# First stage of a transformer-block kernel: low parts of the split to VectorE, scaling and copies to ScalarE, modulation sums one column ahead

## The chip, the cores and the metric

The kernel runs on one core of one Trainium2 chip. The metric is the device time of one execution in microseconds; before the change the median of three runs is 741.49 us (740.28 to 741.51). Engines are named as in the profile: PE (TensorE matmul), PEld (its weight loads), DVE (VectorE), ACT (ScalarE), POOL (GpSimd) and SP (SyncE, which issues most transfers).

## The reference, cut to what matters

One transformer block on 512 tokens of width 1024, in float32. The change lies in the first lines: the modulation from `c`, the normalised input `u`, and the first part of the product with `w_in`.

```python
mod = jax.nn.silu(c) @ w_ada[l] + b_ada[l]
sh1, sc1, g1, sh2, sc2, g2 = [m[:, None, :] for m in jnp.split(mod, 6, axis=-1)]
u = layer_norm(x) * (1 + sc1) + sh1
qa, ka, va, qb, kc, vc, ksl, vsl, kw, vw, gl = jnp.split(u @ w_in[l], split_at, axis=-1)
...
u = layer_norm(x) * (1 + sc2) + sh2
```

`b_ada` holds the bias of the modulation; `1 + sc` and `sh` are a scale and a shift per channel of `u`.

## The kernel before, in words

All float32 products are made of split operands: a raw tile is copied to a rounded high part (`hi`, type fp32r, on ACT, line 256), the low part is `raw - hi` (line 257, on the engine that the caller names), and each product is three matmuls, high by high, high by low and low by high (`mm3`, lines 259 to 262).

**The start.** The vector `c` is loaded as a row, spread over 128 partitions by two matmuls (line 288) and put through Silu into `crow` (line 289). The same vector as columns, `ccol`, is loaded on ACT's queue (line 274) and put through Silu on ACT ahead of `crow` (line 290); `ccol` is used only much later, for `g1` and `g2`. The four token tiles of `x` (128 x 1024 each) get their statistics on DVE (`bn`, `ag`, lines 294 to 302), the power and the offset `nb` on POOL (lines 296, 310, 311), and are normalised in place on ACT (line 336); of the fourth tile, 384 of 1024 columns are done on DVE (line 334).

**The first stage** is the loop at line 372 over `KD = 8` columns `j` of 128 channels of `u`. For each column:

- `ada_cols(j)` (lines 344 to 355) loads the weights of the scale and the shift of these 128 channels as four tiles `ada` of 128 x 512 (256 KB each) and reduces each against a half of `crow` on DVE (line 351, CUSTOM_DVE_ANT_0 in the profile, with an accumulator read behind it). The two halves and the bias are added by line 353, once for the scale and once for the shift, and line 355 adds 1 to the scale.
- `w_first[j]` (128 x 792, 396 KB) is loaded to `wraw`, copied to `whi` on ACT, and its low part `wlo` is made on POOL (`split(w, wh, wl, P)`). `whi` and `wlo` have two buffers each, `wraw` four, `ada` sixteen.
- The normalised `x` is transposed on PE (`x_turn`, line 364, column 0 before the loop's body goes on, columns 1 to 7 within the turn of column 0). The PSUM result is copied to `xTs` on ACT for the even columns and on DVE for the odd ones (lines 367 and 369; `XA = (0, 2, 4, 6)`).
- DVE scales and shifts `xTs` with the column's scale and shift (line 387), ACT copies the result to the high part of `u` (line 256), and DVE makes the low part (line 257).
- PE does 24 matmuls of 256 columns into the banks `first` (line 398) and 12 of 280 columns into the banks `comp` (lines 260 to 262): 36 per column.

Behind the loop PE goes on with the banks `quad` (the rest of `w_in`), and ACT and DVE empty `first` and `comp`. A tile scheduler sets the order of each engine's instructions from the program, the pools and the semaphores; each engine works through its own list in order.

Of the kernel before, what the change touches and what calls it, by code (L numbers as in the profile page):

```python
# [10 lines left out]
F32 = mybir.dt.float32  # L11
# [95 lines left out]
def body(ctx, tc, nc, a, out, dbg=None):  # L107
# [27 lines left out]
    LU = 2  # L135
    TP = 832
    XO = 1
    XV = 1
    X3 = 384
    XW = 0  # L140
    XE = 1
    HP = 0
    FS = 1
    QS = 1
    XA = (0, 2, 4, 6)
    WM = (12, 10)
    PW = 1
    WF = 1
# [49 lines left out]
    def wraw(shape=(128, 1024)):  # L198
        return slot('wr', NR, list(shape), F32, 'wraw')
# [71 lines left out]
        load(xt[t], a['x'][128 * t:128 * t + 128, :])  # L271
    ident = const('ident', [128, 128], A)
    bcol = const('b_col', [128, 4, KD], A)
    ccol = const('ccol', [128, KD], A)
    nhalf = cst.tile([128, 1], F32, name='nhalf')
    V.memset(nhalf, -0.5)
    mone = cst.tile([128, 1], F32, name='mone')
# [8 lines left out]
    for h in range(2):  # L286
        pr = bank('tr', 'cb')
        T.matmul(pr, ones[0:1, :], c1[h][0:1, :], start=True, stop=True)
        A.activation(crow[:, 512 * h:512 * h + 512], pr, AF.Silu)
    A.activation(ccol, ccol, AF.Silu)  # L290

    def rstd_of(st):
        ag = cst.tile([128, 4], F32, name='ag', tag='ag', bufs=4)
# [20 lines left out]
    def warm(n):  # L314
        if n:
            pw = bank('acc', 'warm')
            for _ in range(n):
                T.matmul(pw[:, 0:128], ones, ones, start=True, stop=True)
    for t in range(NT):
        if HP & 1:  # L320
            ctx2 = ExitStack()
            ctx2.enter_context(tc.high_priority())
        y = xt[t]
        ag = stats(y)
        if t in N0P:
            P.tensor_scalar(y, y, ag[:, 0:1], ag[:, 3:4], op0=ALU.subtract, op1=ALU.mult)
        else:
            nb = offset_of(ag, P if NBP else V)
            cs = [slice(0, 1024)]
            if t == 3:  # L330
                cs = [slice(0, X3), slice(X3, 1024)]
                if XV:
                    c = cs.pop(0)
                    V.tensor_scalar(y[:, c], y[:, c], ag[:, 0:1], ag[:, 3:4], op0=ALU.subtract, op1=ALU.mult)
            for c in cs:
                A.activation(y[:, c], y[:, c], AF.Identity, bias=nb, scale=ag[:, 3:4])
        if HP & 1:
            ctx2.close()
    warm(WM[1])


    mod = cst.tile([128, 4, KD], F32, name='mod')

    def ada_cols(j):
        for s in range(2):
            part = cst.tile([128, 2], F32, name='part', tag='part', bufs=4)
            for h in range(2):
                hs = slice(512 * h, 512 * h + 512)
                w = to('ada', F32)
                load(w, a['ada_col'][j, s][:, hs])  # L350
                V.tensor_tensor_reduce(w, w, crow[:, hs], 1.0, 0.0, op0=ALU.mult, op1=ALU.add,
                                       accum_out=part[:, h:h + 1])
            V.scalar_tensor_tensor(mod[:, s, j:j + 1], part[:, 0:1], part[:, 1:2], bcol[:, s, j:j + 1],
                                   op0=ALU.add, op1=ALU.add)
        V.tensor_scalar_add(mod[:, 0, j:j + 1], mod[:, 0, j:j + 1], 1.0)


    _, uh, ul = u_parts()
# [2 lines left out]
    def x_turn(j):  # L361
        pt = bank('tr', 'xT')
        for t in range(NT):
            T.transpose(pt[:, 128 * t:128 * t + 128], xt[t][:, 128 * j:128 * j + 128], ident)
        xT.append(t2('xTs', F32))
        if j in XA:
            A.activation(xT[j], pt, AF.Copy)
        else:
            V.tensor_copy(xT[j], pt)
    accs = [[bank(tg, 'first') for _ in range(2)] for tg in ('acc', 's')]  # L370
    NC1 = 512 + 280
    for j in range(KD):
        if j == 0 and XW:
            w = wraw((128, NC1))
            load(w, a['w_first'][j])
        ada_cols(j)
        if j > 0 or not XW:
            w = wraw((128, NC1))
            load(w, a['w_first'][j])
        wh, wl = whl((128, NC1))  # L380
        if j == 0 and XE:
            x_turn(0)
        split(w, wh, wl, P)
        if j == 0 and not XE:
            x_turn(0)
        y = xT[j]
        V.tensor_scalar(y, y, mod[:, 0, j:j + 1], mod[:, 1, j:j + 1], op0=ALU.mult, op1=ALU.add)
        h_, l_ = uh[j], ul[j]
        split(y, h_, l_, V)
        terms = [[(h_, wh)], [(l_, wh)], [(h_, wl)]] if j == 0 and XO else [[(h_, wh), (h_, wl), (l_, wh)]]  # L390
        for term in terms:
            for i in range(2):
# [626 lines left out]
    def ada_late_cols(gap, which=(2, 3)):  # L1019
        for i in which:  # L1020
            for j in range(KD):
                w = wgem()
                load(w, a['ada_col'][j, i])
                yield gap
                V.tensor_tensor_reduce(w, w, crow, 1.0, 0.0, op0=ALU.mult, op1=ALU.add, accum_out=mod[:, i, j:j + 1])
            V.tensor_add(mod[:, i, :], mod[:, i, :], bcol[:, i, :])
            if i == 2:
                V.tensor_scalar_add(mod[:, 2, :], mod[:, 2, :], 1.0)

    def ada_row(s, out_, gap=None):  # L1030
        res = []
# [525 lines left out]
```

## Time and profile before

| what | before |
|---|---|
| median of three runs | 741.49 us (740.28 to 741.51) |
| the profiled execution's own time | 741.5 us |
| its span, first to last instruction | 739.4 us |
| PE busy, share of the span | 694.3 us, 94% |
| DVE busy | 469.7 us, 64% |
| ACT busy | 338.0 us, 46% |
| POOL busy | 297.1 us, 40% |
| mean granted TensorE clock | 0.99 of full speed |

The span is shorter than the execution's time by 2.1 us, which lie around the first and the last instruction. Busy time counts an instruction from its start to its end, so two that overlap in the pipeline count twice in a mean duration; the distance from one start to the next is what a row of equal instructions costs. A wait is shown as idle time in square brackets, with what ended it.

### The profile page before, as it was taken

What the parts mean: (1) busy time and instruction counts of PE and PEld (TensorE: products, weight loads), DVE (VectorE), ACT (ScalarE), POOL (GpSimd) and SP (SyncE); (2) the same over time, 40 slices, a digit from 0 to 9 for tenths busy, and PEclk for the clock granted to TensorE, in tenths of its full rate; (3) what the DMA queues carried; (4) which work ended last, traced back from release to release, by engine and by line L of the source; (5) the groups of instructions that cost most, each with busy time, mean ns of one, the idle gap of its engine ahead of it and who ended that gap; (6) DMA issues with size and microseconds to landing.
All of it is one profiled execution on the core that took longest, in us unless ns stands there. A gap on an engine that the chain in (4) does not pass through costs nothing.

```text
span 739.4 us, 10876 instructions
## 1 busy us (share of the span) xinstructions
PE 694.3 (94%) x3964; PEld 596.2 (81%) x3964; DVE 469.7 (64%) x969; ACT 338.0 (46%) x685; POOL 297.1 (40%) x303
## 2 busy tenths in 40 slices
PE   7889799999789988999999999999999999999995
PEld 6788678987678977878898888888888888888884
DVE  6998985666788699989854344464543443434336
ACT  4225575664557678963654333433433332223101
POOL 3334583937446628432202011011011147676216
PEclk7999999999999999999999999999999999999998
DMA  8952632134644003080102223344342225343002
GB/s 309 387 186 91 219 125 86 59 110 175 228 139 148 30 29 115 1 275 39 58 27 68 107 86 132 126 147 162 122 138 87 91 83 166 116 141 117 28 15 99
DMA packets 29149, 89.93 MB, mean 122 GB/s; under 512 B 3748, under 2 KB 4516, under 8 KB 29096
## 3 DMA queue, kind: packets, MB, share of 16 engines
q1 hardware_dynamic: 28516, 89.05, 34.6%
q8 instruction: 31, 0.51, 0.3%
q10 hardware_dynamic: 580, 0.19, 0.1%
q14 instruction: 22, 0.18, 0.1%
HBM read 87.13 MB, written 2.10 MB: 121 GB/s over the span
## 4 chain that ended last, share of the span: by engine, by line
PE 50%; DVE 3%; POOL 1%; issue 1%; ACT 0%; POOLq 0%; DVEq 0%
PE d L260 5%; PE d L262 5%; PE d L261 5%; PE pvv L261 5%; PE pvv L260 5%; PE pvv L262 5%; PE pg L261 5%; PE pg L260 5%; PE pg L262 5%; DVE x L1366 1%; PE wo L262 0%; PE wo L261 0%; PE wo L260 0%; DVE x L1357 0%; DVE bn L302 0%
## 5 line engine op out<-in xcount | busy, mean ns | idle before, releaser
L257 DVE TENSOR_TENSOR wlo<-wraw,whi 128x1024 fp32r<-128x1024 f32 x60 | 79.1, 1320 | 122.2 <-ACT whi L256 121.1
L256 ACT ACTIVATE whi<-wraw 128x1024 fp32r<-128x1024 f32 (+1 forms) x68 | 70.4, 1036 | 140.9 <-PE pg L261 68.3
L260 PE MATMUL quad<-whi,u 128*128 128x256 f32 x256 | 75.1, 294 | 2.2 <-DVE kll L481 1.2
L261 PE MATMUL quad<-wlo,u 128*128 128x256 f32 x256 | 72.5, 283 | 0.2 <-POOL wlo L1122 0.2
L262 PE MATMUL quad<-whi,u 128*128 128x256 f32 x256 | 72.4, 283 | 0.0
L1509 POOL TENSOR_TENSOR wraw<-wraw,arow 128x1024 f32<-128x1024 f32 x22 | 61.0, 2790 | 24.3 <-DMA wraw<-w_down 23.1
L257 POOL TENSOR_TENSOR hl<-cv,hh 128x512 fp32r<-128x512 f32 x14 | 22.3, 1596 | 119.7 <-ACT hh L256 119.7
L260 PE MATMUL pg<-u,whi 128*128 128x512 f32 (+1 forms) x176 | 67.7, 384 | 0.0
L261 PE MATMUL pg<-u,whi 128*128 128x512 f32 (+1 forms) x176 | 66.8, 379 | 0.0
L262 PE MATMUL pvv<-u,wlo 128*128 128x512 f32 (+1 forms) x176 | 66.8, 379 | 0.0
L262 PE MATMUL pg<-u,wlo 128*128 128x512 f32 (+1 forms) x176 | 66.8, 379 | 0.0
L260 PE MATMUL pvv<-u,whi 128*128 128x512 f32 (+1 forms) x176 | 66.8, 379 | 0.0
L261 PE MATMUL pvv<-u,whi 128*128 128x512 f32 (+1 forms) x176 | 66.8, 379 | 0.0
L1122 POOL TENSOR_TENSOR wlo<-wraw,whi 128x512 fp32r<-128x512 f32 x32 | 48.3, 1530 | 27.1 <-ACT whi L1119 27.0
L260 PEld LDWEIGHTS quad<-whi,u 128*128 128x128 f32 x256 | 48.5, 190 | 7.3 <-issue 3.9
L710 DVE CUSTOM_DVE_ANT_0 p<-sp,masks 128x128 f32<-128x128 f32 (+1 forms) x96 | 45.0, 483 | 8.9 <-PE sp L703 8.5
L261 PEld LDWEIGHTS quad<-wlo,u 128*128 128x128 f32 x256 | 48.6, 190 | 1.1 <-POOL wlo L1122 0.4
L262 PEld LDWEIGHTS quad<-whi,u 128*128 128x128 f32 x256 | 48.6, 190 | 0.1
L729 PE MATMUL pT<-ident,p 128*128 128x128 f32 x240 | 39.9, 279 | 4.9 <-POOL p L724 4.6
L257 POOL TENSOR_TENSOR hg<-cv,hg 128x512 fp32r<-128x512 f32 x8 | 12.7, 1590 | 75.3 <-ACT hg L256 75.3
L260 PEld LDWEIGHTS pg<-u,whi 128*128 128x128 f32 x176 | 33.1, 188 | 6.6 <-issue 0.5
L261 PEld LDWEIGHTS pg<-u,whi 128*128 128x128 f32 x176 | 33.1, 188 | 6.6 <-issue 0.5
(637 smaller groups left out, 1910.3 us busy)
## 6 DMA issues: line engine op xcount, KB each, us to landing
wraw<-w_up SPq DMA_DIRECT2D x44, 512.0 KB, 3.2
wraw<-w_down SPq DMA_DIRECT2D x22, 512.0 KB, 3.2
ada<-ada_col SPq DMA_DIRECT2D x32, 256.0 KB, 6.1
wraw<-w_quad SPq DMA_DIRECT2D x16, 512.0 KB, 4.1
wraw<-ada_col SPq DMA_DIRECT2D x16, 512.0 KB, 4.1
wraw<-ada_row SPq DMA_DIRECT2D x16, 512.0 KB, 3.2
x<-x SPq DMA_DIRECT2D x8, 512.0 KB, 6.0
wraw<-w_o SPq DMA_DIRECT2D x8, 512.0 KB, 3.7
```

The lines of the kernel that those rows point to most:

```text
L256: A.activation(hi, raw, AF.Copy)
L257: lo_engine.tensor_sub(lo, raw, f(hi))
L260: T.matmul(o_, sh, mh, start=start, stop=False)
L261: T.matmul(o_, sh, ml, start=False, stop=False)
L262: T.matmul(o_, sl, mh, start=False, stop=stop)
L710: V.tensor_tensor_reduce(p[:, cols[i]], e['s'][:, cols[i]], masks[:, m0:mask0 + 512], 1.0, 3e38, op0=ALU.add, op1=ALU.min, accum_out=m_[:, ...
L729: T.transpose(e['t'][:, 128 * j:128 * j + 128], e['p'][:, 128 * j:128 * j + 128], ident)
L1122: P.tensor_sub(wl[:, p:p + PS], w[:, p:p + PS], f(wh[:, p:p + PS]))
L1366: V.scalar_tensor_tensor(src[:, hs], src[:, hs], ag[:, 3:4], b_[h][:, cs], op0=ALU.mult, op1=ALU.add)
L1509: P.tensor_mul(w, w, g2)
```

## The change

The low part `wlo` of `w_first` is made on DVE and no longer on POOL. The reductions take a starting value from memory: the first half of `crow` starts from the bias (`bcol`, to which 1 is added once, in two small instructions, for the two scales), the second half starts from the first one's sum and writes the scale or shift itself, so that lines 353 and 355 go. In the program the four reductions of column j+1 stand within column j: the two of the scale ahead of and around `wlo`, the two of the shift around the low part of `u`. The scaling of `xTs` (line 387) and all copies of the transposed `x` move to ACT; column 0 is scaled straight out of PSUM. The fourth tile of `x` is normalised wholly on ACT (`XV = 0`). `ccol` is loaded at the end of the stage, on SP's queue behind the last `w_first`, and its Silu stands there too. The late columns (line 1025) take the bias as starting value as well.

```diff
-    XV = 1
+    XV = 0
...
-    ccol = const('ccol', [128, KD], A)
...
-    A.activation(ccol, ccol, AF.Silu)
...
+    keep = tc.keep_in_program_order
+    for i in (0, 2):
+        keep(V.tensor_scalar_add(bcol[:, i, :], bcol[:, i, :], 1.0))
...
-    def ada_cols(j):
-        for s in range(2):
-            part = cst.tile([128, 2], F32, name='part', tag='part', bufs=4)
+    def ada_cols(j, which=(0, 1)):
+        for s in which if j < KD else ():
+            part = cst.tile([128, 1], F32, name='part', tag='part', bufs=4)
             for h in range(2):
                 hs = slice(512 * h, 512 * h + 512)
                 w = to('ada', F32)
                 load(w, a['ada_col'][j, s][:, hs])
-                V.tensor_tensor_reduce(w, w, crow[:, hs], 1.0, 0.0, op0=ALU.mult, op1=ALU.add,
-                                       accum_out=part[:, h:h + 1])
-            V.scalar_tensor_tensor(mod[:, s, j:j + 1], part[:, 0:1], part[:, 1:2], bcol[:, s, j:j + 1],
-                                   op0=ALU.add, op1=ALU.add)
-        V.tensor_scalar_add(mod[:, 0, j:j + 1], mod[:, 0, j:j + 1], 1.0)
+                x = V.tensor_tensor_reduce(w, w, crow[:, hs], 1.0, part if h else bcol[:, s, j:j + 1], op0=ALU.mult, op1=ALU.add,
+                                           accum_out=mod[:, s, j:j + 1] if h else part)
+                if j == 0 and s == 0 and h == 0:
+                    keep(x)
...
-        if j in XA:
-            A.activation(xT[j], pt, AF.Copy)
-        else:
-            V.tensor_copy(xT[j], pt)
+        if j == 0:
+            return pt
+        A.activation(xT[j], pt, AF.Copy)
...
-        ada_cols(j)
-        if j > 0 or not XW:
-            w = wraw((128, NC1))
-            load(w, a['w_first'][j])
+        if j == 0:
+            ada_cols(0)
+        w = wraw((128, NC1))
+        load(w, a['w_first'][j])
         wh, wl = whl((128, NC1))
-        if j == 0 and XE:
-            x_turn(0)
-        split(w, wh, wl, P)
-        if j == 0 and not XE:
-            x_turn(0)
+        if j == 0:
+            pt0 = x_turn(0)
+        A.activation(wh, w, AF.Copy)
+        ada_cols(j + 1, (0,))
+        V.tensor_sub(wl, w, f(wh))
         y = xT[j]
-        V.tensor_scalar(y, y, mod[:, 0, j:j + 1], mod[:, 1, j:j + 1], op0=ALU.mult, op1=ALU.add)
+        A.activation(y, pt0 if j == 0 else y, AF.Identity, bias=mod[:, 1, j:j + 1], scale=mod[:, 0, j:j + 1])
         h_, l_ = uh[j], ul[j]
-        split(y, h_, l_, V)
+        hi_ = A.activation(h_, y, AF.Copy)
+        ada_cols(j + 1, (1,))
+        V.tensor_sub(l_, y, f(h_))
...
-            for jj in range(1, KD):
-                x_turn(jj)
+            with tc.issue_after(hi_.ins):
+                for jj in range(1, KD):
+                    x_turn(jj)
...
+    ccol = const('ccol', [128, KD])
+    A.activation(ccol, ccol, AF.Silu)
...
-                V.tensor_tensor_reduce(w, w, crow, 1.0, 0.0, op0=ALU.mult, op1=ALU.add, accum_out=mod[:, i, j:j + 1])
-            V.tensor_add(mod[:, i, :], mod[:, i, :], bcol[:, i, :])
-            if i == 2:
-                V.tensor_scalar_add(mod[:, 2, :], mod[:, 2, :], 1.0)
+                V.tensor_tensor_reduce(w, w, crow, 1.0, bcol[:, i, j:j + 1], op0=ALU.mult, op1=ALU.add, accum_out=mod[:, i, j:j + 1])
```

The program's line order alone does not tell where the instructions stand, so two places of the engines' lists follow. The first is DVE at a column in the middle of the stage (L351 and L349 with `ada` are the reductions, the row behind each its accumulator read). Before:

```order
L351 ISA ada_615,part_614<-ada_615,crow_88 128x512
L351 ISA part_614 128x1
L353 SCALAR_TENSOR_TENSOR mod_165<-part_606,b_col_78 128x1
L351 ISA ada_618,part_614<-ada_618,crow_88 128x512
L351 ISA part_614 128x1
L355 TENSOR_SCALAR mod_165<-mod_165 128x1
L353 SCALAR_TENSOR_TENSOR mod_165<-part_614,b_col_78 128x1
L387 TENSOR_SCALAR xTs_271<-xTs_271,mod_165 128x512
L351 ISA ada_669,part_668<-ada_669,crow_88 128x512
L351 ISA part_668 128x1
L257 TENSOR_TENSOR u_169<-xTs_271,u_167 128x512
```

The same place with the change:

```order
L349 ISA ada_370,part_369<-ada_370,crow_86,b_col_78 128x512
L349 ISA part_369 128x1
L378 TENSOR_TENSOR wlo_367<-wraw_364,whi_366 128x792
L349 ISA ada_373,mod_164<-ada_373,crow_86,part_369 128x512
L349 ISA mod_164 128x1
L349 ISA ada_380,part_379<-ada_380,crow_86,b_col_78 128x512
L349 ISA part_379 128x1
L384 TENSOR_TENSOR u_167<-xTs_252,u_165 128x512
L349 ISA ada_383,mod_164<-ada_383,crow_86,part_379 128x512
L349 ISA mod_164 128x1
```

The three small additions and the scaling are gone from DVE's list, the low part `wlo` has come in, and each pair of reductions has a low part between its halves. POOL's list loses its eight `wlo` of this stage and is otherwise the same.

The second place is ACT at the start, from the table load on. Before:

```order
L290 ACT_TABLE_LOAD
L290 ACTIVATE ccol_80<-ccol_80 128x8
L289 ACTIVATE crow_88<-cb_102 128x512
L289 ACTIVATE crow_88<-cb_105 128x512
L336 ACTIVATE x_68<-x_68,nb_116,ag_112 128x1024
L336 ACTIVATE x_70<-x_70,nb_127,ag_123 128x1024
L336 ACTIVATE x_72<-x_72,nb_138,ag_134 128x1024
L336 ACTIVATE x_74<-x_74,nb_149,ag_145 128x640
L367 ACTIVATE xTs_200<-xT_195 128x512
L256 ACTIVATE whi_193<-wraw_191 128x792
L367 ACTIVATE xTs_243<-xT_238 128x512
L256 ACTIVATE u_166<-xTs_200 128x512
```

With the change:

```order
L287 ACT_TABLE_LOAD
L287 ACTIVATE crow_86<-cb_100 128x512
L287 ACTIVATE crow_86<-cb_103 128x512
L332 ACTIVATE x_68<-x_68,nb_124,ag_120 128x1024
L332 ACTIVATE x_70<-x_70,nb_135,ag_131 128x1024
L332 ACTIVATE x_72<-x_72,nb_146,ag_142 128x1024
L332 ACTIVATE x_74<-x_74,nb_157,ag_153 128x384
L332 ACTIVATE x_74<-x_74,nb_157,ag_153 128x640
L376 ACTIVATE whi_189<-wraw_187 128x792
L380 ACTIVATE xTs_196<-xT_191,mod_164 128x512
L382 ACTIVATE u_165<-xTs_196 128x512
L365 ACTIVATE xTs_245<-xT_240 128x512
```

`ccol` no longer stands ahead of `crow`, the fourth tile of `x` is there in two pieces, and column 0 goes from `whi` straight to the scaling and the high part of `u`; the copies of the other columns follow behind it, four ahead of the next `whi` and three behind the next high part of `u`.

## Rows read from the trace of the kernel before

**Rows 1.** Busy time by stretch, 5 us each: PE, PEld, DVE, ACT, POOL, PEclk, DMA, GB/s

```profile
0.00:5.00 5.00, 3.89 (x22) 3.89 (x23) 1.40 (x6) 1.28 (x1) 0.20 (x4) 1.00 0.64 227
...
20.00:25.00 5.00, 5.00 (x39) 4.78 (x37) 5.00 (x12) 1.20 (x2) 1.88 (x1) 0.90 1.05 389
...
55.00:60.00 5.00, 4.28 (x33) 4.07 (x34) 4.91 (x12) 1.20 (x2) 2.25 (x1) 1.00 0.17 45
```

**Rows 2.** Timeline of DVE, two columns of the stage: start us, duration us, instruction

```profile
35.04 1.85 DVE L353 SCALAR_TENSOR_TENSOR mod<-part,b_col 128x1 f32<-128x1 f32 x1
...
49.59 0.69 DVE L257 TENSOR_TENSOR u<-xTs,u 128x512 fp32r<-128x512 f32 x1
...
50.81 2.38 DVE L351 CUSTOM_DVE_ANT_0 ada<-ada,crow 128x512 f32<-128x512 f32 x1
...
53.98 0.22 DVE L353 SCALAR_TENSOR_TENSOR mod<-part,b_col 128x1 f32<-128x1 f32 x1
54.24 0.55 DVE L387 TENSOR_SCALAR xTs<-xTs,mod 128x512 f32<-128x512 f32 x1
...
55.48 0.69 DVE L257 TENSOR_TENSOR u<-xTs,u 128x512 fp32r<-128x512 f32 x1
```

**Rows 3.** Timeline of POOL in the same two columns

```profile
34.66 2.22 POOL L257 TENSOR_TENSOR wlo<-wraw,whi 128x792 fp32r<-128x792 f32 x1 [3.26 <-DMA ada<-ada_col]
...
50.39 2.26 POOL L257 TENSOR_TENSOR wlo<-wraw,whi 128x792 fp32r<-128x792 f32 x1 [2.96 <-ACT whi L256]
```

**Rows 4.** Timeline of PE, last column and what follows it

```profile
61.39 0.39 PE L398 MATMUL first<-whi,u 128*128 128x256 f32 x1 [0.74 <-ACT u L256]
...
62.57 0.40 PE L398 MATMUL first<-whi,u 128*128 128x256 f32 x2
...
64.85 0.29 PE L260 MATMUL comp<-whi,u 128*128 128x280 f32 x1
...
66.38 0.28 PE L260 MATMUL quad<-whi,u 128*128 128x256 f32 x1
```

**Rows 5.** Timeline of the start, all engines

```profile
5.33 1.98 PE L288 MATMUL cb<-c,ones 1*128 1x512 f32 x4
...
11.15 4.31 ACT L336 ACTIVATE x<-x,nb,ag 128x1024 f32<-128x1024 f32 x4
...
12.36 0.93 POOL L296 TENSOR_TENSOR ag<-ag,nhalf 128x1 f32<-128x1 f32 x1
...
13.37 0.19 POOL L311 TENSOR_TENSOR nb<-nb,ag 128x1 f32<-128x1 f32 x1
...
18.86 2.06 PE L398 MATMUL first<-whi,u 128*128 128x256 f32 x8
```

**Rows 6.** Groups of ACT's instructions, 3 to 66 us: busy us, mean ns | idle before

```profile
L256 ACT ACTIVATE whi<-wraw 128x792 fp32r<-128x792 f32 x8 | 6.9, 858 | 2.2 <-PE comp L262 1.5 <-DMA wraw<-w_quad 0.7
L256 ACT ACTIVATE u<-xTs 128x512 fp32r<-128x512 f32 x8 | 5.0, 630 | 25.5 <-DVE xTs L387 25.5
L336 ACT ACTIVATE x<-x,nb,ag 128x1024 f32<-128x1024 f32 x3 | 3.5, 1234 | 0.0
...
L336 ACT ACTIVATE x<-x,nb,ag 128x640 f32<-128x640 f32 x1 | 0.9, 911 | 0.0
...
L290 ACT ACTIVATE ccol<-ccol 128x8 f32<-128x8 f32 x1 | 0.2, 209 | 5.8 <-DMA ccol<-ccol 5.8
```

**Rows 7.** Busy time by stretch of 1 us: as Rows 1, the clock behind the engines

```profile
20.00:21.00 1.00, 1.00 (x7) 1.00 (x6) 1.00 (x3) 0.60 (x1) 0.32 (x1) 0.50 1.03 394
21.00:22.00 1.00, 1.00 (x10) 1.00 (x9) 1.00 (x1) 0.00 (x0) 1.00 (x1) 0.99 1.06 393
```

**Rows 8.** Line 257 by tile, whole span: duration ns min/median/max

```profile
L257 DVE TENSOR_TENSOR wlo<-wraw,whi x60: 1209/1226/3156, 324.5 to 699.6; 128x1024 fp32r<-128x1024 f32 x60
...
L257 DVE TENSOR_TENSOR u<-xTs,u x8: 674/688/693, 20.1 to 61.4; 128x512 fp32r<-128x512 f32 x8
```

**Rows 9.** Busy time by stretch of 10 us, behind the first stage

```profile
90.00:100.00 10.00, 7.59 (x52) 6.61 (x52) 9.74 (x34) 5.83 (x19) 9.53 (x12) 1.00 0.40 144
```

More of the change, by code (lines that the diff above doesn't have):

```diff
@@ L144, in body @@
     QS = 1
-    XA = (0, 2, 4, 6)
     WM = (12, 10)
@@ L318, in warm @@
                 T.matmul(pw[:, 0:128], ones, ones, start=True, stop=True)
+    warm(WM[1])
     for t in range(NT):
@@ L324, in body @@
         ag = stats(y)
-        if t in N0P:
-            P.tensor_scalar(y, y, ag[:, 0:1], ag[:, 3:4], op0=ALU.subtract, op1=ALU.mult)
-        else:
+        if True:
             nb = offset_of(ag, P if NBP else V)
@@ L338, in body @@
             ctx2.close()
-    warm(WM[1])
+    keep = tc.keep_in_program_order
+    for i in (0, 2):
+        keep(V.tensor_scalar_add(bcol[:, i, :], bcol[:, i, :], 1.0))
     mod = cst.tile([128, 4, KD], F32, name='mod')
-    def ada_cols(j):
-        for s in range(2):
-            part = cst.tile([128, 2], F32, name='part', tag='part', bufs=4)
+    def ada_cols(j, which=(0, 1)):
+        for s in which if j < KD else ():
+            part = cst.tile([128, 1], F32, name='part', tag='part', bufs=4)
             for h in range(2):
@@ L365, in x_turn @@
         xT.append(t2('xTs', F32))
-        if j in XA:
-            A.activation(xT[j], pt, AF.Copy)
-        else:
-            V.tensor_copy(xT[j], pt)
+        if j == 0:
+            return pt
+        A.activation(xT[j], pt, AF.Copy)
     accs = [[bank(tg, 'first') for _ in range(2)] for tg in ('acc', 's')]
@@ L372, in body @@
     for j in range(KD):
-        if j == 0 and XW:
-            w = wraw((128, NC1))
-            load(w, a['w_first'][j])
-        ada_cols(j)
-        if j > 0 or not XW:
-            w = wraw((128, NC1))
-            load(w, a['w_first'][j])
-        wh, wl = whl((128, NC1))
-        if j == 0 and XE:
-            x_turn(0)
-        split(w, wh, wl, P)
-        if j == 0 and not XE:
-            x_turn(0)
+        if j == 0:
+            ada_cols(0)
+        w = wraw((128, NC1))
+        load(w, a['w_first'][j])
+        wh, wl = whl((128, NC1))
+        if j == 0:
[3 more added lines that the diff above has]
+        V.tensor_sub(wl, w, f(wh))
         y = xT[j]
-        V.tensor_scalar(y, y, mod[:, 0, j:j + 1], mod[:, 1, j:j + 1], op0=ALU.mult, op1=ALU.add)
+        A.activation(y, pt0 if j == 0 else y, AF.Identity, bias=mod[:, 1, j:j + 1], scale=mod[:, 0, j:j + 1])
         h_, l_ = uh[j], ul[j]
-        split(y, h_, l_, V)
+        hi_ = A.activation(h_, y, AF.Copy)
+        ada_cols(j + 1, (1,))
+        V.tensor_sub(l_, y, f(h_))
         terms = [[(h_, wh)], [(l_, wh)], [(h_, wl)]] if j == 0 and XO else [[(h_, wh), (h_, wl), (l_, wh)]]
```

## The prediction

> **What bounds the kernel now.** I read three views in this order. First the busy time by stretch [rows 1]. In the first 60 us DVE is the engine without a gap (5.00 of 5.00 us at 20 to 25, 4.91 at 55 to 60), while PE, which owns the rest of the kernel, is at 4.28. The transfers run full until about 40 us (389 GB/s) and are nearly idle at 55 us (45 GB/s), so the end of the stage is not theirs. Then DVE's timeline [rows 2]: from one low part of `u` to the next, 49.59 to 55.48, is 5.89 us. An addition on one number per partition takes 0.22 us at 53.98, but 1.85 at 35.04; a reduction takes 2.38 us at 50.81, although 49.59 to 50.81 holds a low part of `u` and a whole reduction, so 0.61 us is what one of 512 columns costs. Last POOL's timeline [rows 3]: `wlo` runs from 34.66 to 36.88 and the addition at 35.04 ends at 36.89; `wlo` runs from 50.39 to 52.65 and the reduction ends at 53.19, one reduction's time later. All eight `wlo` of the stage lie so over a stretched DVE instruction. DVE stands still for about 1.7 us per column while POOL works. PE waits for `u` at each column, 0.74 us at the last [rows 4], and ACT waits 25.5 us in all for DVE's scaling [rows 6]. PE's own need is less than 5.89: 62.57 to 64.85 are 19 matmuls, 0.12 us each, and 64.85 to 66.38 the 12 of `comp`, 1.53 us, so a column costs 24 x 0.12 + 1.53 = **4.41 us** [rows 4]. The stage ends for PE at 66.38 [rows 4].
>
> **The change part by part.**
>
> *DVE per column.* `wlo` comes in. Low parts on DVE take 0.688 us at 512 columns and 1.226 at 1024 [rows 8]; 792 lies on the line at 0.98, about 0.95 start to start. The scaling (0.46), three small additions (0.13 to 0.26 each) and the 1.7 us of standing still go. Left are 4 x 0.61 + 0.95 + 0.61 = 4.0 us against PE's 4.41. The one unseen price is that a reduction starts from a value in memory. Below: nothing, and I exclude a gain, as the instruction has the same work. Above: 0.26 us each, the distance at which a small instruction that needs its predecessor's result follows it (53.98 to 54.24 [rows 2]). I take nothing: the first half's sum is written a whole low part before the second half reads it, and the bias long before. The upper end makes 5.0 us per column and is a rival below.
>
> *ACT per column.* `whi` 0.86, high part of `u` 0.63 [rows 6], and the scaling with two operands per partition. Such an instruction takes 0.911 us at 640 columns and 1.234 at 1024 [rows 6], so 0.80 at 512. 2.3 us of 4.41: covered. If this cover went, PE would wait for the high part first.
>
> *The loop over two `whi` buffers.* `whi` of column j waits until PE is done with column j-2. Behind it come `wlo` 0.95, two reductions 1.22 and the low part of `u` 0.69: 0.86 + 0.95 + 1.22 + 0.69 = 3.72 us, in which PE does column j-1 for 4.41. The margin is 0.7 us, and PE stays the bound. Who waits on whom there: the low part of `u` now stands behind a reduction of the next column's weights, and PE behind that.
>
> *Transfers.* A column needs 4 x 256 + 396 = 1420 KB, 1.454 MB; at 389 GB/s [rows 1] that is 3.74 us, less than 4.41. SP's list keeps its order; `ccol` stands behind the last `w_first`, where the queue has room, and it is read again only after 60 us. The late columns lose a few small DVE additions, which I cost at nothing.
>
> *The start.* ACT waited 5.8 us for `ccol` [rows 6]; without it `crow` follows the matmuls that end at 7.31 [rows 5], and three tiles of `x` at 1.23 us or less are done by about 12. The fourth needs its offset, 13.37 + 0.19 = 13.56 before [rows 5]; DVE no longer puts reductions ahead of its statistics (about 0.9 us) and the power takes less than its 0.93 [rows 5]. I take 12.2, with 13.56 as the other end. The tile's 1024 columns in two pieces, about 1.35 (1.234 plus a second start), end at 13.55; 384 of them were DVE's. By then 3.55 MB are in (5 us at 227 GB/s, then 389 [rows 1], makes 11.2 us), so `w_first` is there. Then 0.86 + 0.80 + 0.63 to 15.9, and the first product of `u` at 16.2, behind four transposes, instead of 18.86 [rows 5]. The other end, 1.3 later, would be partly paid back below, since the slow-clock part of column 0 shrinks.
>
> *Column 0.* On PE there are 24 + 12 matmuls, the 20 transposes of columns 3 to 7 and one matmul of column 1: 45 x 0.12 + 1.53 = 6.9 us at full clock. The granted clock was 0.50 (1.2 GHz) at 20 to 21 us and 0.99 from 21 [rows 7], after some 5 us of unbroken transposes and matmuls; I let it rise at 21 again. From 16.2 to 21 half the time is lost, 2.4 us, so column 0 ends at 16.2 + 6.9 + 2.4 = 25.5. ACT puts four copies of transposed columns ahead of the second `whi`; they wait for transposes on PE, `whi` ends near 21.5, `wlo` 22.5, the low part of `u` 24.4, all before 25.5. The rise bounds this term: each us earlier or later is half a us; I allow 17 to 24, that is -2.0 to +1.5.
>
> *The sum.* 25.5 + 7 x 4.41 = 56.4, against 66.38: **10.0 us**. What follows starts from PE's last column in both kernels and is released by buffers, not by the clock on the wall, so I carry all of it to the end: 741.5 of the profiled execution, which is also the median of the runs, less 10.0 is **731.5 us**.
>
> **The rivals.**
>
> *Part of the lead is given back later.* Behind the stage PE is not alone: at 90 to 100 us it is busy 7.59 of 10 us, DVE 9.74 and POOL 9.53 [rows 9]. For it: DVE is nearly full there, and a few instructions change places. Against: DVE's work there starts from the banks that PE fills, so it moves along, and transfers have room (144 GB/s [rows 9]). Giving back 3 to 5 us makes 734.5 to 736.5.
>
> *A starting value costs 0.26 us.* DVE's column is then 5.0 us and sets the pace for six columns: 6 x 0.6 = 3.5 us lost, 735. Against it: nothing in the list lets a reduction start from the one just ahead of it.
>
> *DVE's standing still is its own.* Then the 1.7 us stay, and a column costs 5.89 - 0.46 - 0.5 + 0.95 = 5.9 us as before; only the earlier start is gained, 2.6 us: 738.9. The Trainium skill (Perfetto Trace Analysis, Optimizing Scalar/DVE Operations) speaks for this side: with DVE saturated it may pay to put work on ScalarE or even GpSimd, and this change takes work from GpSimd back to a full DVE. The same section adds that the two share an SBUF read port, so that such moves might not help. By that rule's first half the time would be 738.9, by the rows 731.5. For the rows: both stretched instructions that I show end with POOL's `wlo` or one reduction's time behind it [rows 2, 3].
>
> *Slower: the next column's loads hold the low part of `u`.* A late reduction of column j+1 now delays PE in column j. If a column's loads take L, the stage loses 7 x (L - 4.41) once they set the pace, and all of the 10.0 us at L = 5.84, that is 1.454 MB at 249 GB/s. At the 227 GB/s of the first 5 us [rows 1] L is 6.4, the loss 13.9 and the time 745.4. For it: the buffers come free in a new order, on DVE instead of POOL. Against: 389 GB/s were seen in the stage [rows 1], and `wraw` comes free earlier than before.
>
> **How the numbers follow.** I give my forecast 0.77 (729 to 734: clock, the offset's two ends, 1 us of rearranged instructions), the lead partly given back 0.11, the dearer reduction 0.06, DVE's own standing still 0.03, slower 0.03. The predicted time is the likeliest case. The range from 728.5 to 736 holds the forecast's bounds, the dearer reduction and most of the give-back. Less than 0.2% either way, 1.5 us, is what a measurement of this kernel can tell from no change. All cases but the last two are faster by more; DVE's own standing still is mostly faster by more, too, but near the bound, so I split it: faster 0.94, same 0.03, slower 0.03.
>
> **What would show it right or wrong.** Right: no DVE instruction over 1.3 us between 12 and 50 us, DVE with gaps in the second half of the stage, PE without waits over 0.3 us from column 1 on at 4.4 us per column, the first product of `u` near 16 us and the first `quad` near 56. Wrong: reductions above 0.75 us start to start, PE waiting for `u` or for `whi` in every column, a clock of 0.50 beyond 24 us, or a first `quad` near 56 with an end later than 734.

## The result and the profile after

| | before | after |
|---|---|---|
| median of four runs | 741.50 us (740.28 to 742.17) | 733.95 us (733.58 to 734.93) |
| ratio, 95% interval | | 0.9902 [0.9885, 0.9919] |
| the profiled execution | 741.5 us | 733.94 us |
| its span | 739.4 us | 732.2 us |

The time fell by 7.5 us. The forecast was 10.0 us and 731.5 us; the range, 728.5 to 736, holds the result. The first stage did what was forecast and half a us more, and some 3 us were lost behind it.

**The stage.** Busy time by stretch, 5 us each, answering [rows 1]: PE, PEld, DVE, ACT, POOL, PEclk, DMA, GB/s.

```profile
20.00:25.00 5.00, 5.00 (x39) 4.63 (x38) 4.26 (x10) 3.73 (x6) 0.00 (x0) 0.94 1.05 387
55.00:60.00 5.00, 5.00 (x43) 5.00 (x43) 4.30 (x14) 1.71 (x3) 1.29 (x1) 1.00 0.34 116
```

PE is busy without a gap and DVE has gaps (4.26 of 5), the reverse of before. Now DVE's timeline over half a column, answering [rows 2]:

```profile
34.87 0.98 DVE L378 TENSOR_TENSOR wlo<-wraw,whi 128x792 fp32r<-128x792 f32 x1
35.77 0.74 DVE L349 CUSTOM_DVE_ANT_0 ada<-ada,crow,part 128x512 f32<-128x512 f32 x1
...
36.44 0.75 DVE L349 CUSTOM_DVE_ANT_0 ada<-ada,crow,b_col 128x512 f32<-128x512 f32 x1
```

`wlo` takes 0.98 us, as interpolated. Between 12 and 53 us no instruction of DVE is stretched; the longest is `wlo`. The reductions at 35.77 and 36.44 stand 0.67 us apart, not 0.61. POOL does nothing from 11.8 to 53.5 us; its next row answers [rows 3]:

```profile
53.53 1.30 POOL L1117 TENSOR_TENSOR wlo<-wraw,whi 128x512 fp32r<-128x512 f32 x1 [41.78 <-DVE rt L426]
```

PE's timeline, the first matmul of two neighbouring columns and the first `quad`, answering [rows 4]:

```profile
33.77 0.28 PE L393 MATMUL first<-whi,u 128*128 128x256 f32 x1
...
38.18 0.28 PE L393 MATMUL first<-whi,u 128*128 128x256 f32 x1
...
55.84 0.28 PE L259 MATMUL quad<-whi,u 128*128 128x256 f32 x1
```

Each column from the third on costs 4.41 us (the second, of which one matmul lies in the first, 4.30), and none holds a wait. The first `quad` starts at 55.84 where it was 66.38: a lead of 10.5 us. The start, answering [rows 5, 6], in the timeline of ACT, POOL and PE:

```profile
7.85 0.60 ACT L287 ACTIVATE crow<-cb 128x512 f32<-128x512 f32 x1 [4.13 <-PE cb L286]
...
9.21 4.91 ACT L332 ACTIVATE x<-x,nb,ag 128x1024 f32<-128x1024 f32 x5
...
14.77 0.76 ACT L380 ACTIVATE xTs<-xT,mod 128x512 f32<-128x512 f32 x1
...
11.41 0.35 POOL L308 TENSOR_TENSOR nb<-nb,ag 128x1 f32<-128x1 f32 x1
...
16.25 1.37 PE L393 MATMUL first<-whi,u 128*128 128x256 f32 x8
```

`crow` no longer waits for `ccol`, the fourth tile's offset is there at 11.76, and the first product of `u` starts at 16.25. In the windows of 1 us, answering [rows 7], the clock was at 0.50 from 18 to 20 us and full from 21:

```profile
18.00:19.00 1.00, 1.00 (x8) 1.00 (x6) 1.00 (x3) 0.49 (x1) 0.00 (x0) 0.50 1.04 388
...
21.00:22.00 1.00, 1.00 (x11) 1.00 (x10) 1.00 (x2) 0.97 (x2) 0.00 (x0) 1.00 1.13 411
```

**Behind the stage** the lead shrinks: 10.5 us at the first `quad`, 6.2 at the first score (`sp`, 86.14 before, 79.98 after), 6.7 at the product of the row `g1` (`gr`, 193.0 and 186.3) and 7.2 at the end of the span. The timelines of ACT, POOL, PE, SP and DVE show where it went:

```profile
54.30 0.64 ACT L1114 ACTIVATE whi<-wraw 128x512 fp32r<-128x512 f32 x1
58.27 0.66 ACT L548 ACTIVATE yc<-comp 128x256 f32<-128x256 f32 x2 [3.32 <-DVE gates L539]
58.95 1.28 ACT L540 ACT_TABLE_LOAD   x1
...
60.96 1.67 ACT L1114 ACTIVATE whi<-wraw 128x512 fp32r<-128x512 f32 x3
...
61.67 6.99 POOL L1117 TENSOR_TENSOR wlo<-wraw,whi 128x512 fp32r<-128x512 f32 x4 [5.35 <-ACT whi L1114]
...
63.83 0.39 PE L260 MATMUL quad<-wlo,u 128*128 128x256 f32 x1 [1.30 <-POOL wlo L1117]
...
66.04 0.38 PE L260 MATMUL quad<-wlo,u 128*128 128x256 f32 x1 [1.22 <-POOL wlo L1117]
...
74.76 0.77 PE L462 MATMUL qT<-ident,yq 128*128 128x128 f32 x4 [3.77 <-DVE yq L427]
...
68.69 4.84 SPq L240 DMA_DIRECT2D wraw<-ada_col  x2
...
71.88 1.28 DVE L1023 CUSTOM_DVE_ANT_0 wraw<-wraw,crow,b_col 128x1024 f32<-128x1024 f32 x1 [5.62 <-DMA wraw<-ada_col]
```

ACT's list has changed there, though no edit touches it. Two copies of `yc` now stand behind the second `quad` `whi` and wait 3.32 us for DVE, and the third `whi` (in the row at 60.96) stands behind them. Before, the third `whi` came first, in ACT's timeline of the kernel before:

```profile
66.63 0.63 ACT L1119 ACTIVATE whi<-wraw 128x512 fp32r<-128x512 f32 x1 [1.12 <-issue]
67.28 1.28 ACT L542 ACT_TABLE_LOAD   x1
```

So POOL's third low part begins 5.8 us after the first `quad` instead of 1.0. PE waits 1.3 and 1.2 us for low parts; the buffers of POOL's four low parts come free late, so SP issues a late column's load at 68.69; DVE stands 5.62 us for that load with the rotation of `yq` in its list behind it, and PE waits 3.77 us for that rotation. Right behind that wait PE's granted clock is at half of full, from 75.2 to 78.6 us, in stretches of 1 us:

```profile
75.00:76.00 1.00, 1.00 (x8) 1.00 (x7) 0.99 (x5) 0.74 (x2) 0.00 (x0) 0.58 0.70 266
76.00:77.00 1.00, 1.00 (x6) 1.00 (x6) 0.97 (x4) 0.98 (x2) 0.00 (x0) 0.50 0.00 0
```

### The profile page after: what moved, and what is told of

It reads as the page before. It is cut to its first block, busy times and chain, and to the rows that moved or that the text cites. A ratio compares the mean times of both kernels' runs of the same rounds, so it can differ in the third digit from the quotient of the medians.

```text
span 732.2 us, 10862 instructions
## 1 busy us (share of the span) xinstructions
PE 691.7 (94%) x3964; PEld 596.0 (81%) x3964; DVE 454.5 (62%) x939; ACT 346.0 (47%) x697; POOL 275.5 (38%) x295
## 4 chain that ended last, share of the span: by engine, by line
PE 50%; DVE 3%; POOL 1%; issue 1%; ACT 0%; POOLq 0%; DVEq 0%
PE d L260 5%; PE d L259 5%; PE d L261 5%; PE pvv L261 5%; PE pvv L260 5%; PE pvv L259 5%; PE pg L261 5%; PE pg L260 5%; PE pg L259 5%; DVE x L1361 1%; PE wo L259 0%; PE wo L261 0%; PE wo L260 0%; DVE x L1352 0%; DVE bn L299 0%
## 5 line engine op out<-in xcount | busy, mean ns | idle before, releaser
L256 DVE TENSOR_TENSOR wlo<-wraw,whi 128x1024 fp32r<-128x1024 f32 x60 | 85.6, 1429 | 134.9 <-ACT whi L255 133.7
L255 ACT ACTIVATE whi<-wraw 128x1024 fp32r<-128x1024 f32 x60 | 63.7, 1061 | 148.2 <-PE pg L260 72.1
L1504 POOL TENSOR_TENSOR wraw<-wraw,arow 128x1024 f32<-128x1024 f32 x22 | 58.8, 2685 | 27.5 <-DMA wraw<-w_down 25.2
L259 PEld LDWEIGHTS quad<-whi,u 128*128 128x128 f32 x256 | 49.3, 193 | 7.4 <-issue 3.9
L261 PEld LDWEIGHTS quad<-whi,u 128*128 128x128 f32 x256 | 49.3, 193 | 0.0
```

The costliest lines, as they stand in the source:

```text
L255: A.activation(hi, raw, AF.Copy)
L256: lo_engine.tensor_sub(lo, raw, f(hi))
L259: T.matmul(o_, sh, mh, start=start, stop=False)
L261: T.matmul(o_, sl, mh, start=False, stop=stop)
L1504: P.tensor_mul(w, w, g2)
```

## The experiments

Each run is timed beside the kernel before on its chip, where that took 736.98 to 744.86 us in single runs; medians a few us apart need the ratios and their intervals, and where in the program time goes is read from stretches of the profiled execution. Only one execution of each run is profiled, and where the runs of a kernel scatter it need not be a typical one. All of them, with starts from PE's groups by tile (us):

| run | first `quad` | to first score | on to `gr` | on to the end | median | ratio, interval |
|---|---|---|---|---|---|---|
| before | 66.4 | 19.8 | 106.9 | 546.4 | 741.50 | |
| the change | 55.8 | 24.2 | 106.3 | 545.8 | 733.95 | 0.9902 [0.9885, 0.9919] |
| the same again | 54.6 | 23.1 | 107.7 | 546.2 | 735.10 | 0.9912 [0.9886, 0.9939] |
| `wlo` on POOL again | 61.3 | 22.6 | 107.4 | 546.0 | 739.51 | 0.9994 [0.9972, 1.0016] |
| before, `wlo` on DVE | 57.1 | 21.0 | 106.7 | 546.4 | 737.26 | 0.9951 [0.9924, 0.9978] |
| constant start | 57.2 | 22.7 | 107.6 | 546.1 | 735.38, one run | |
| `ccol` at the start | 56.9 | 18.8 | 111.8 | 546.6 | 735.83 | 0.9901 [0.9868, 0.9935] |
| higher priority | 55.7 | 20.5 | 111.2 | 546.5 | 734.46 | 0.9914 [0.9889, 0.9939] |
| copies behind exponential | 55.9 | 20.0 | 111.3 | 545.6 | 733.68 | 0.9888 [0.9867, 0.9909] |
| the same, second run | 55.7 | 19.6 | 107.9 | 547.5 | 732.59 | 0.9885 [0.9848, 0.9921] |
| and one copy on POOL | 55.9 | 19.9 | 106.4 | 545.7 | 730.69 | 0.9860 [0.9831, 0.9889] |
| scaling on DVE | 56.4 | 18.6 | 107.7 | 546.1 | 731.91 | 0.9890 [0.9853, 0.9927] |
| the same, second run | 55.0 | 19.2 | 107.9 | 546.4 | 731.09 | 0.9861 [0.9833, 0.9890] |

The last stretch is the same within 2 us everywhere. Most of the differences are made in the first three.

**Does POOL hold DVE up?** Two runs ask it, from both sides.

```diff
-        V.tensor_sub(wl, w, f(wh))
+        P.tensor_sub(wl, w, f(wh))
```

> The changed kernel with one line put back: the low part of the first stage's chunk is made by POOL again (all else as changed, ACT's order at the stage's end too). Theory, that POOL's low part keeps DVE standing: one reduction of each column should be 1.7 us longer again than the others, as in the kernel before (2.38 against 0.68), so DVE's column is 4 x 0.67 + 0.60 + 1.7 = about 5.0 instead of 4.41, the first quad product comes 7 x 0.6 = 4 us later, near 60 us, and the time is 737 to 739. Rival, that DVE's time was its own work and the long reduction was slow for a reason of its own: DVE has 0.9 us less of work in a column, PE's 4.41 a column stays, the first quad stays at 55.8, the time at 733.9 or below.

The timelines of DVE, POOL and ACT in one column of this run, and POOL's next `wlo`:

```profile
32.72 1.97 DVE L384 TENSOR_TENSOR u<-xTs,u 128x512 fp32r<-128x512 f32 x1 [0.69 <-ACT u L382]
...
32.25 1.90 POOL L378 TENSOR_TENSOR wlo<-wraw,whi 128x792 fp32r<-128x792 f32 x1 [3.70 <-ACT whi L376]
37.84 1.89 POOL L378 TENSOR_TENSOR wlo<-wraw,whi 128x792 fp32r<-128x792 f32 x1 [3.70 <-ACT whi L376]
...
31.32 0.85 ACT L376 ACTIVATE whi<-wraw 128x792 fp32r<-128x792 f32 x1
32.08 0.61 ACT L382 ACTIVATE u<-xTs 128x512 fp32r<-128x512 f32 x1
```

DVE does stand, for 1.28 us (1.97 against 0.69), but at the low part of `u`, not at a reduction. A column costs 5.59 us (32.25 to 37.84), where 5.0 was expected, the first `quad` comes 5.5 us late, and by the runs the whole gain is gone (0.9994). Not all of the 5.59 is DVE standing: the edit also changed ACT's order, so that `whi` lies between the scaling and the high part of `u`, and DVE waits 0.69 us for the latter. So this run shows what the line is worth, and the next one, from the other side, shows why more cleanly.

```diff
-        split(w, wh, wl, P)
+        split(w, wh, wl, V)
```

> The kernel before with one edit: the low part of the first stage's chunk on DVE in place of POOL; the reductions, the scaling and the start stay as before. Theory, that DVE stood still for POOL: the long reduction (2.38) falls to 0.68 and 0.9 us of subtraction come in, so DVE's column goes from 5.89 to about 5.1, the first quad comes 7 x 0.8 = 5.6 us earlier, near 61 us, and the time is 736 to 738 (ACT's order after the stage has the third quad half behind the compressed keys' copies here too, so a part is given back). Rival, that DVE was full of work of its own: the column becomes 5.89 + 0.9 = 6.8, the first quad 72 to 73, the time 747 to 748.

DVE's timeline, two low parts of neighbouring columns:

```profile
35.78 0.97 DVE L257 TENSOR_TENSOR wlo<-wraw,whi 128x792 fp32r<-128x792 f32 x1
...
40.51 0.96 DVE L257 TENSOR_TENSOR wlo<-wraw,whi 128x792 fp32r<-128x792 f32 x1
```

The column is 4.73 us with 0.9 us more work on DVE, where it was 5.89, and from 16 to 54 us no instruction of DVE takes over 0.98 us. The rival's 6.8 us is refuted. The first `quad` at 57.1 is 9.3 us earlier than before, more than expected; 2.3 us of that are there at the first product (16.58 against 18.86). But this profile is of the shortest of ten executions (733.03 us; the others up to 740.57, the longer ones at a mean granted clock of 0.980 to 0.985 against 0.992 here). By the median and its ratio, 0.9951, this line alone brings about half of what the whole change brings (0.9902), and the two intervals do not overlap.

**The price of a starting value.**

```diff
-                x = V.tensor_tensor_reduce(w, w, crow[:, hs], 1.0, part if h else bcol[:, s, j:j + 1], ...
+                x = V.tensor_tensor_reduce(w, w, crow[:, hs], 1.0, 0.0, ...
...
+            V.scalar_tensor_tensor(mod[:, s, j:j + 1], part[:, 0:1], part[:, 1:2], bcol[:, s, j:j + 1], ...
```

> The changed kernel with the first stage's reductions started from the constant 0 again and their halves and the bias added by one operation a column and part. By the price of the pointer (0.67 start to start against 0.61 in the kernel before): the reductions are at 0.61 again, 4 x 0.06 = 0.24 us less in a column, and the two additions take 0.10 to 0.14 each, so DVE's work of a column stays near 4.2, PE's 4.41 a column and the first quad near 55.8 stay as they are. If the 0.67 come from something else of the changed stage (PE or DMA reading and writing at the same time), the reductions stay at 0.67.

```profile
33.60 0.69 DVE L349 CUSTOM_DVE_ANT_0 ada<-ada,crow 128x512 f32<-128x512 f32 x1
...
34.21 0.69 DVE L386 TENSOR_TENSOR u<-xTs,u 128x512 fp32r<-128x512 f32 x1
```

In this DVE timeline a reduction from a constant takes 0.61 us again (33.60 to 34.21). So the starting value costs 0.06 us each, whether bias or first half. The first product came at 17.6 us in this run, as DVE waited 1.64 us for a tile of `x`, and that is the later first `quad`. From there to the first `quad` the time is the changed kernel's (17.6 to 57.2 and 16.25 to 55.84 are both 39.6 us), but not column by column: three of the columns took 4.57 us where 4.41 was expected, and the first one was as much shorter.

**The start.**

```diff
+    ccol = const('ccol', [128, KD], A)
...
+    A.activation(ccol, ccol, AF.Silu)
...
-    ccol = const('ccol', [128, KD])
-    A.activation(ccol, ccol, AF.Silu)
```

> The changed kernel with one part undone: column c is loaded at the start again, on ACT's queue, and its Silu stands ahead of the two of row c. Behind the stage ACT's order is that of the kernel before again, unasked. Term of the start: the Silus of row c wait for column c to 10.1 us as in the kernel before, ACT's first scaling of x starts 1.9 us later, and the first product comes 1.5 to 2 us later, near 18, the first quad near 57.5. Theory of the order: the end's lead over the kernel before is that of the first quad within 1.5 us, so the time is 731.5 to 733. Rival: no effect of the order, 735.5 to 736.

The Silu of `ccol` started at 9.22 us, ACT's first `x` at 10.29 instead of 9.21, and the first product at 17.4: the term is 1.1 us, less than the 1.5 to 2 expected, since `ccol` landed earlier than before. The old order of ACT came back with it, and the stretch to the first score is 18.8 us. The time is a miss, though: 735.83, because the next stretch took 111.8 us.

**The order on ACT.** Three runs restore it behind an unchanged stage, or nearly so. The first raises the priority of the first quad's copies:

```diff
-                    A.activation(wh[:, 2 * p:2 * p + 2], w[:, 2 * p:2 * p + 2], AF.Copy)
+                    with tc.high_priority() if i == 0 else ExitStack():
+                        A.activation(wh[:, 2 * p:2 * p + 2], w[:, 2 * p:2 * p + 2], AF.Copy)
```

> The changed kernel with one edit behind the first stage: the copies of the first quad's weight halves get a higher priority, so that ACT makes all four of them ahead of the gates' exponential and the compressed columns' copies, where the changed kernel made the third and fourth 5 us later. Theory, that this order is where the lead went from 10.5 to 7 us: POOL's third low part starts near 57 instead of 61.67, PE's two waits for it (1.2 and 1.3 us) go, the column's transfer that DVE waited 5.6 us for is issued some 3 to 4 us earlier and the transposes behind it come as much earlier, the scores' lead over the kernel before is 9 to 10 us, and the time is 730.5 to 731.5. Rival, that the lead was lost to the transfers or to the clock's fall near 75 us whatever the order: 733.5 to 734.5, with the same wait of DVE for the column.

The second holds the copies of `yc` back:

```diff
-    A.activation(gates, gates, AF.Exp, scale=-1.0)
+    ge = A.activation(gates, gates, AF.Exp, scale=-1.0)
...
+            with tc.issue_after(ge.ins):
+                A.activation(y[:, t], cacc[2 * b + t][:, 0:256].rearrange("p (h d) -> p h d", d=64), AF.Copy)
```

> The changed kernel with one edit behind the first stage: the compressed columns' copies are kept behind the gates' exponential on ACT, which gives ACT the order of the kernel before (the third quad half ahead of the table load); from the scores on the instructions stand in the changed kernel's order. Theory, that this order cost the lead: the first quad stays at 55.8, the scores come 3 to 4 us earlier than 80.0 and, since nothing behind them is reordered, the gain is kept to the end: about 3 us below the changed kernel beside it, 730 to 731.5 where that takes 734. Rival, from the run with raised priority (scores 3.8 us earlier, end no earlier): the lead is given back later by a transfer that comes at its own time, the wait for the row that PE had at 186 us grows, and the time is within 1 us of the changed kernel's.

The third puts the scaling back on DVE, after which the scheduler sets the old order by itself:

```diff
-        A.activation(y, pt0 if j == 0 else y, AF.Identity, bias=mod[:, 1, j:j + 1], scale=mod[:, 0, j:j + 1])
+        V.tensor_scalar(y, pt0 if j == 0 else y, mod[:, 0, j:j + 1], mod[:, 1, j:j + 1], op0=ALU.mult, op1=ALU.add)
```

> The changed kernel with the scaling of the turned input put back on DVE. Two things move: DVE's column grows by 0.46 (the scaling in the kernel before, start to start) from 4 x 0.67 + 0.90 + 0.60 = 4.2 to 4.64, which would be 0.23 us a column over PE's 4.41, so the first quad should come 1 to 2 us later than 55.8; and ACT's order behind the stage is that of the kernel before again, with the third quad half ahead of the gates. Theory of the order: the lead over the kernel before at the end is within 1.5 us of the lead at the first quad, so the time is 731 to 733, no slower than the changed kernel though its stage is longer. Rival, that the order behind the stage doesn't count: 735 to 736.

> The kernel with the scaling on DVE again, beside the changed kernel on one chip: by the first run of it (first quad 56.4, scores 75.0, end 728.8) it should be 2 to 4 us below the changed kernel, and within 1 us of the one with the copies behind the exponential. If its first time was chance, it is within 1 us of the changed kernel.

> The changed kernel itself once more, as the measure for the runs beside it on this chip: 7 to 8 us below the kernel before, with the first quad product near 55.8, the scores near 80.0 and DVE's wait of 5.6 us for a column's transfer near 72 us.

The first half of the theory holds in every run: with the third `whi` ahead of the table load and the copies of `yc` behind it the stretch to the first score is 18.6 to 20.5 us, with the changed order 22.6 to 24.2 (21.0 in the kernel before with `wlo` on DVE, where the third `whi` comes first but three copies of `yc` stand ahead of the table load). ACT and POOL with the copies held back:

```profile
56.10 0.63 ACT L1115 ACTIVATE whi<-wraw 128x512 fp32r<-128x512 f32 x1 [1.08 <-PE comp L261]
56.75 1.28 ACT L540 ACT_TABLE_LOAD   x1
...
56.81 1.29 POOL L1118 TENSOR_TENSOR wlo<-wraw,whi 128x512 fp32r<-128x512 f32 x1 [0.43 <-ACT whi L1115]
```

The second half, that this gain is kept, fits the scaling on DVE alone: 0.9861 beside 0.9912 for the change on the same chip, though the two intervals just touch, and its first run (0.9890, against 0.9902 for the change) tells no difference. The DVE column there is 4.76 us, over PE's 4.41, and yet the kernel is no slower and likely faster. The other two are misses (734.46 and 733.68, where 730.5 to 731.5 and 730 to 731.5 were expected). In these two, and with `ccol` at the start, the lead was lost again by the product of the row: 111 to 112 us from the first score to `gr`, where ten other profiles have 106 to 108. PE's waits in this stretch are 10.1 to 11.2 us in these three and 6.0 to 7.5 in the ten. The change's own second run came 6.1 us below the kernel before, not 7 to 8, with the same wait of DVE (5.61 us).

**The second loss.** The timelines of DVE, POOL and PE in the kernel with the copies held back:

```profile
173.37 2.38 DVE L1015 SCALAR_TENSOR_TENSOR arow<-wraw,ccol,arow 128x1024 f32<-128x1024 f32 x1 [2.58 <-DMA wraw<-ada_row]
...
183.33 1.35 DVE L524 TENSOR_TENSOR gxz<-gxz 128x124 f32<-128x124 f32 x1
184.71 1.17 DVE L525 TENSOR_SCALAR gxz<-gxz 128x124 f32<-128x124 f32 x1
...
173.41 3.49 POOL L1118 TENSOR_TENSOR wlo<-wraw,whi 128x512 fp32r<-128x512 f32 x2 [2.78 <-ACT whi L1115]
...
182.92 2.88 POOL L1118 TENSOR_TENSOR wlo<-wraw,whi 128x512 fp32r<-128x512 f32 x2 [0.55 <-ACT whi L1115]
...
187.15 2.04 PE L1038 MATMUL gr<-arow,ones 128*128 128x512 f32 x2 [4.59 <-DVE arow L1033]
```

Its 10 us from 180 in the view of stretches:

```profile
180.00:190.00 10.00, 5.41 (x29) 4.10 (x29) 7.84 (x11) 3.40 (x7) 5.17 (x7) 0.73 0.67 226
```

The same timelines in the second run with the scaling on DVE:

```profile
171.53 1.29 DVE L1014 SCALAR_TENSOR_TENSOR arow<-wraw,ccol,arow 128x1024 f32<-128x1024 f32 x1 [2.67 <-DMA wraw<-ada_row]
...
180.30 0.28 DVE L524 TENSOR_TENSOR gxz<-gxz 128x124 f32<-128x124 f32 x1
...
171.62 3.56 POOL L1117 TENSOR_TENSOR wlo<-wraw,whi 128x512 fp32r<-128x512 f32 x2 [2.94 <-ACT whi L1114]
...
182.11 1.10 PE L1037 MATMUL gr<-arow,ones 128*128 128x512 f32 x2 [1.38 <-DVE arow L1032]
```

DVE adds up the row `g1` (`arow`) from loads that share their buffers with the weights, while POOL makes low parts. At 171.53 DVE began 0.09 us ahead of POOL and took 1.29 us; at 173.37 both began within 0.04 us and DVE took 2.38. From there it grows: the buffer is free 1.1 us later and the next loads come as much later; then POOL's next low part is ahead of two short instructions of DVE (1.35 and 1.17 instead of 0.28 and 0.23). PE waits 4.59 us for the row instead of 1.38, and its granted clock falls to 0.73 of full over these 10 us. The three profiles with a slow sum here (1.99 to 2.38; POOL ahead by 0.35 and 0.16, or within 0.04) are the three with 111 to 112 us; where DVE was ahead by 0.09 us or more the sum took 1.28 or 1.29. From the start of this sum to `gr` the three take 13.3 to 13.8 us and the ten 10.5 to 10.7, so some 3 us are lost between these two places. If that is the cause, making POOL later must make the kernel faster:

```diff
+                    if (i, c, p) == (3, 0, 0):
+                        spare = cst.tile([128, 64], F32, name='spare')
+                        P.tensor_copy(spare, f(wh[:, 0, 0:64]))
                     P.tensor_sub(wl[:, p:p + PS], w[:, p:p + PS], f(wh[:, p:p + PS]))
```

> The kernel with the compressed columns' copies behind the exponential, and one instruction more on POOL: a copy of 128 x 64 numbers to a tile that nothing reads, ahead of the low part near 173 us (the seventh quad chunk's first), so that this low part starts about 0.3 us later; nothing else is moved. Theory, that the lead was lost there because POOL's low part began in the same moment as DVE's sum of the row: with POOL 0.3 us behind, DVE's sum takes 1.28 again in place of 2.38, the next transfers of the row come 1.1 us earlier, DVE's two short operations near 183 us are ahead of POOL's next low part (0.28 and 0.23 in place of 1.35 and 1.17), PE waits 1.4 us for the row in place of 4.6 and its granted clock stays at full speed, the stretch from the first score to the row's product is 107 to 108 us in place of 111, and an instruction more makes the kernel some 3 to 4 us faster: 729.5 to 731. Rival, that the lead drains because the row's transfers come at their own pace: the same wait of 4 us or more and 733 to 734.

> The same kernel without the extra copy, beside it on one chip: 733 to 734, with the sum near 173 us at 2 us or more and PE's wait of 4 us for the row. If here DVE's sum should happen to start 0.1 us or more ahead of POOL's low part, the theory has it at 1.28 and this run as fast as the one with the copy.

The timelines of POOL, DVE and PE in the kernel with the copy:

```profile
173.04 0.24 POOL L1120 COPY spare<-whi 128x64 f32<-128x64 f32 x1 [2.22 <-ACT whi L1115]
173.25 2.50 POOL L1121 TENSOR_TENSOR wlo<-wraw,whi 128x512 fp32r<-128x512 f32 x2
...
167.11 2.31 DVE L1015 SCALAR_TENSOR_TENSOR arow<-wraw,ccol,arow 128x1024 f32<-128x1024 f32 x1 [1.43 <-DMA wraw<-ada_row]
...
171.73 1.28 DVE L1015 SCALAR_TENSOR_TENSOR arow<-wraw,ccol,arow 128x1024 f32<-128x1024 f32 x1 [0.33 <-DMA wraw<-ada_row]
...
180.25 0.41 DVE L524 TENSOR_TENSOR gxz<-gxz 128x124 f32<-128x124 f32 x1
...
182.19 1.10 PE L1038 MATMUL gr<-arow,ones 128*128 128x512 f32 x2 [0.42 <-DVE arow L1033]
```

and its stretch from 180 us:

```profile
180.00:190.00 10.00, 8.22 (x56) 6.52 (x54) 9.42 (x18) 6.37 (x14) 6.89 (x10) 1.00 0.58 193
```

In the kernel with the copy DVE's sum took 1.28 us, PE waited 0.42 us, the clock was full over these 10 us (it fell for 3.4 us from 208.6) and the stretch was 106.4 us; the time is 730.69, as expected. But this profile does not show the copy at work: the sum began at 171.73 and ended at 173.01, and the copy began at 173.04, so POOL would have come behind the sum without it, too. In its second run, without the copy, the kernel happened to have DVE 0.12 us ahead (172.67 and 172.79), and its stretch was 107.9 us, as expected for that case; 1.9 us more than in the first run went in the last stretch, and its profiled execution took 732.49.

So the same kernel was profiled with the collision (111.3 us) and without it (107.9 us), and all 13 profiles agree on where the 3 us go. That is a strong link, but no run puts the collision in or takes it out, so as a cause it is argued and not shown. The copy's own worth is open: 0.9860 and 0.9885 have overlapping intervals, and the runs scatter from 729.68 to 732.22 with it and from 730.10 to 735.49 without. Nor is a stretched sum always a loss: in the profile with the copy the sum before, at 167.11, took 2.31 us, and the stretch was among the shortest.

## Why the prediction was right, and where it was not

- **DVE stands still for POOL**: right; one line moved from either side shows it, most cleanly in the kernel before. The Trainium skill's rule that I weighed (Perfetto Trace Analysis, Optimizing Scalar/DVE Operations) says that it may make sense to move work off a full DVE, even to GpSimd. Here taking POOL's work back made DVE's column shorter, 5.89 to 4.73 us. Another page of the Trainium skill (SBUF — State Buffer, SBUF: two separate sides) says that an instruction of DVE with two SBUF inputs and one of GpSimd that reads SBUF exclude each other at the port pair that they share, and that whichever starts first keeps it for its whole length. The rows at 32.25 (POOL first, and DVE took 1.97 us) and 171.53 (DVE first by 0.09 us, and it took 1.29) agree; at 173.37 the record has DVE first by 0.04 us, and yet it took 2.38, which the rule by itself does not give.
- **DVE's column** 4.0 us: its work is 4 x 0.67 + 0.90 + 0.60 = 4.2. The starting value, taken at nothing between 0 and 0.26, is 0.06. PE's 4.41 still covers it.
- **PE's column**, 4.41, and ACT's scaling, 0.80: as worked out. The `whi` loop, from `whi` to the end of the low part of `u`, took 3.83 us (33.97 to 37.80) for 3.72.
- **The start**: first product forecast at 16.2, measured 16.25. The offset came at 11.8, not 12.2. The clock was at half speed from 17.1 to 20.6 us, where the sum let it be so from the first product to 21: 1.7 us lost and not 2.4. So the first column ended at 25.06 instead of 25.5. (The sum also counts one matmul of the second column twice, 0.12 us.)
- **The stage's end**: 55.84 against 56.4.
- **"I carry all of it to the end"** is the step that failed. What follows the stage did not start in the same order: ACT's list changed, and 4.2 us of the 10.5 were gone by the first score (24.2 against 20.0 us with the old order). From the first `quad` to the first score PE's waits are 6.3 us with the changed order and 3.6 with the old one (3.2 in the kernel before), and the clock at half speed from 75.2 to 78.6 us costs 1.7 us; two matmuls fewer, 0.24 us, lie in this stretch with the changed order. That is all of the 4.2. The rival "part of the lead is given back later" named instructions that change places, and priced them at 3 to 5 us; it was given 0.11 because I looked at how full DVE is at 90 to 100 us [rows 9], not at the lists between 56 and 80.
- **The number** lies in the range, but by the size of the loss and not by the forecast's reasoning: the course was the forecast's up to the first `quad` and the rival's behind it. Of the prediction's own signs, those of being right came true for the stage. The last sign of being wrong, a first `quad` near 56 with an end later than 734, was missed by 0.05 us (733.95) and met in the second run of the change (735.10).
- Restoring the order does not by itself bring the forecast's 731.5: the medians with it run from 730.69 to 735.83, and the profiles with the collision 100 us later lost some 3 us more. Nothing in the prediction looked there.
- **The chances**: 0.94 for faster is the sum of the first three cases, so the case that DVE's standing still is its own was not split as the text says.

How often the change alone meets the collision stays open; its two profiles show DVE ahead by 0.27 and 0.12 us.

## What to carry to other kernels

Where two engines stretch each other, price the move by what stands still and not by the instruction's own time: 0.9 us of added work made a full DVE 1.16 us faster per column. A lead won in one stage is only carried if the next stage's lists are the same, so compare them on every engine as far as the first instruction that everything waits for. And a lead that shifts two engines against each other can meet a coincidence much later; look for the next instruction that suddenly takes another one's length longer, and check in the profile that an edit meant to avoid it was at work there before crediting it.

## What the hardware showed unexpectedly

- A reduction that starts from a value per partition in memory takes 0.67 us start to start at 512 columns, from a constant 0.61.
- A few hundredths of a us between the starts of DVE and POOL go with a sum of 1.28 us or one of up to 2.38: DVE was 0.06 us ahead at 166.45 in the first run with the scaling on DVE (1.28 us), 0.04 ahead at 173.37 (2.38 us), 0.05 behind at 167.11 (2.31 us).
- It is not always the same instruction that stands still for POOL: in the kernel before a reduction and a one-number addition [rows 2], with `wlo` back on POOL the low part of `u`, behind the stage a sum of 1024 columns.
